# Building a gate table from one-hot pairs: one float32 VectorE operation per eight tokens, a stepped PSUM tile, and 62 parked chunks in place of 48

## The chip, the cores and the metric

The kernel runs on one core of a Trainium2 chip. The engines are TensorE (PE for its matmuls, PEld for its weight loads), VectorE (DVE), ScalarE (ACT), GpSimd (POOL) and SyncE (SP, which here issues the plain DMAs). The metric is the device time of one execution in microseconds, lower is better.

## The reference, cut to what matters

One encoder block over 512 tokens of width 1024. What this text is about is its last big part, a product-key retrieval over 128 x 128 = 16384 single-neuron experts, 8 heads with 16 experts each, so that every token has 128 experts and 128 gates:

```python
top_s, pos = lax.top_k(cand, K)
idx = jnp.take_along_axis(cand_idx, pos, axis=-1)      # i1 * 128 + i2
g = jax.nn.softmax(top_s, axis=-1)
...
ue = jnp.take(u, ib, axis=0)
a = jnp.einsum('thkd,td->thk', ue, xb)
w = jax.nn.gelu(a) * gb
ve = jnp.take(v, ib, axis=0)
return jnp.einsum('thk,thkd->td', w, ve)
```

## The kernel before, in words

The first third of the program (input projections, attention, the recurrent branch, the merge) is not touched. Then the 512 tokens of the retrieval are split: the first 128 are done as the reference does it, with gathered rows of u and v (an indirect DMA on the POOL queue, then a DVE product: `gu`, `gv`, lines 885, 891, 900). The other 384 tokens are done densely: for all 16384 experts, in 128 chunks of 128 experts, the kernel computes gelu(u x), multiplies it with a gate table that is zero where an expert was not chosen, and multiplies the result with v.

A **chunk** on the first side is `dense_a` (line 776 on): one load of 512 KB (`u_raw`), its split into two parts (`u_h` on ACT, line 139; `u_l` on DVE, line 140), 24 matmuls of 128 x 384 into the PSUM tile `pa` (lines 134 to 136), and a Gelu on ACT to `ge` (line 784). On the second side (`w_prep` and `w_mm`) a chunk takes the split of `v_raw`, a product with the gate table (line 1003), a split into `w_h` and `w_l`, and 18 matmuls of 128 x 512 into `po`.

**The gate table** has for each of the 384 tokens a 128 x 128 matrix: entry (i, j) is the gate of expert 128 i + j. `build` makes it as a product of two one-hot matrices. For a block of 128 tokens the chosen i, j and gates are transposed (`tij`, `gr`: token along the free axis, choice along the partitions). Then, for 8 tokens at a time (`TQ`):

- DVE compares: `gL` (line 865), 8 x 128 float32, from a constant `iob` that holds 0..127 in bfloat16 with every value 8 times in a row, read with a step; and `gO` (line 867), 128 x 8 bfloat16, with the 8 tokens innermost;
- ACT scales one token's slice of `gO` by the gates into `gR` (line 869), one instruction for each token, which reads with a step of 8 elements;
- PE multiplies `gR` and `gL` of one token into `pg` (line 874), four tokens in a PSUM tile, each with its 128 columns side by side. A float32 matmul of the program is two matmul instructions in the profile, so there are 768 of them for 384 tokens;
- ACT copies `pg` to `gs` (line 876) and turns it there, so that the token is innermost.

After 32 tokens (`GB`), `gs` (one buffer) goes to memory in one DMA of 2 MB (line 878): 12 such blocks in all, four for each of the three blocks of 128 tokens.

While the table is not finished, no `po` matmul can run. So the table's work is interleaved with `dense_a` of the first `SP` chunks, whose results are **parked** in memory (`adram<-ge`, line 958) and read back in the last stage (`ges<-adram`). The other 128 - `SP` chunks are **fresh**: their `dense_a` is done among the `po` matmuls of the last stage. Generators set the program order: `units()` zips the selection of the experts (`sel`, `topk`: many small DVE operations) of one block with the `build` of another, each step with a cost; whenever the cost passes another multiple of `APACE`, one more `dense_a` is issued (`next_a`), and the gathers come in at a pace of their own (`GPACE`). A scheduler then places the instructions of each engine; each engine and each DMA queue runs its own in that order.

Of the kernel before, what the change touches and what calls it, by code (L numbers as in the profile page):

```python
# [8 lines left out]
F32 = mybir.dt.float32  # L9
F32R = mybir.dt.float32r  # L10
BF16 = mybir.dt.bfloat16
I32 = mybir.dt.int32
U32 = mybir.dt.uint32
AF = mybir.ActivationFunctionType
OP = mybir.AluOpType
# [31 lines left out]
TD = T - NG  # L47
NTB = TD // GB
PRE = 8
SP = 48  # L50
TQ = 8
APACE = 3.3
GPACE = 0.4
GSTART = 30
GS2 = 135
# [22 lines left out]
def chunk_order():  # L78
    spilled, fresh = [], []
    for c in range(128):  # L80
        ns, nf = SP - len(spilled), 128 - SP - len(fresh)
        (spilled if ns and (c < S0 or not nf or ns * (128 - SP) >= nf * SP) else fresh).append(c)
    return {c: i for i, c in enumerate(spilled)}, spilled + fresh
# [29 lines left out]
def zipped(*gens):  # L113
    gens = [[0.0, i, g] for i, g in enumerate(gens)]
    while gens:
        e = min(gens)
        try:
            c = next(e[2])
        except StopIteration:
            gens.remove(e)  # L120
            continue
        e[0] += c
        yield c
# [633 lines left out]
def peer(nc, tc, I, out, xd, cst, gains, norm_T1, rstd_of, split, mm3, tap, stop, pp, ha, la, h2n, v8s, i8s, st, top,  # L757
         idxg, gg, acc, aa, ul_st, up, u_split, u_pre):
    import contextlib
    V, S, PE, G, DM = nc.vector, nc.scalar, nc.tensor, nc.gpsimd, nc.sync  # L760
    ident = cst[:, C_ID:C_ID + 128]
    iota = cst[:, C_IOTA:C_IOTA + 128]
# [3 lines left out]
    if True:  # L766
        dp = st.enter_context(tc.tile_pool(name="gdram", bufs=1, space=bass.MemoryType.DRAM))
        gd = dp.tile([NTB, 128, 128 * GB], F32, name="gdram")
        ad = dp.tile([SP, 128, TD], F32, name="adram")
        ys = contextlib.ExitStack()  # L770
# [76 lines left out]
            V.tensor_tensor(g3, g3, sm[:, :, None].to_broadcast([128, 8, 16]), op=OP.mult)  # L847
            yield 0.6

        def build(kp, bp, ps, tb, i_f, g_o, iob):  # L850
            pt = ps.tile([128, 3, 128], F32, name="pt3", tag="pt3", bufs=1)
            for i, s in enumerate((i_f[:, 0, :], i_f[:, 1, :], g_o)):
                PE.transpose(pt[:, i, :], s, ident)
            tij = kp.tile([128, 2, 128], BF16, name="tij", tag="tij")
            S.activation(tij, pt[:, 0:2, :], AF.Copy)
            gr = kp.tile([128, 128], F32, name="gr", tag="gr")
            S.activation(gr, pt[:, 2, :], AF.Copy)
            for b in range(128 // GB):
                gs = bp.tile([128, 128, GB], F32, name="gs", tag="gs", bufs=1)
                for q8 in range(GB // TQ):  # L860
                    t0 = b * GB + q8 * TQ
                    LL = bp.tile([128, TQ, 128], F32, name="gL", tag="gL")
                    OO = bp.tile([128, 128, TQ], BF16, name="gO", tag="gO")
                    RR = bp.tile([128, TQ, 128], F32, name="gR", tag="gR")
                    V.tensor_tensor(LL, iob[:, :, 0][:, None, :].to_broadcast([128, TQ, 128]),
                                    tij[:, 0, t0:t0 + TQ, None].to_broadcast([128, TQ, 128]), op=OP.is_equal)
                    V.tensor_tensor(OO, iob, tij[:, 1, None, t0:t0 + TQ].to_broadcast([128, 128, TQ]), op=OP.is_equal)  # L867
                    for t in range(TQ):
                        S.activation(RR[:, t, :], OO[:, :, t], AF.Copy, scale=gr[:, t0 + t:t0 + t + 1])  # L869
                    for q4 in range(TQ // 4):  # L870
                        pg = ps.tile([128, 4, 128], F32, name="pg", tag="pg")
                        for w in range(4):
                            t = q4 * 4 + w
                            PE.matmul(pg[:, w, :], RR[:, t, :], LL[:, t, :], start=True, stop=True)  # L874
                        o = q8 * TQ + 4 * q4
                        S.activation(gs[:, :, o:o + 4].rearrange("p i t -> p t i"), pg, AF.Copy)  # L876
                    yield TQ * 0.21 + 0.1
                DM.dma_start(gd[(tb - TB0) * (128 // GB) + b], gs.rearrange("p i t -> p (i t)"))

# [40 lines left out]
        with s7:  # L920
            kp = s7.enter_context(tc.tile_pool(name="topk", side="right", **LR))
            bp = s7.enter_context(tc.tile_pool(name="gbld", side="right", bufs=2, reuse_waits="tile"))
            ps = s7.enter_context(tc.psum_pool(name="psg", side="right", bufs=2, reuse_waits="tile"))
            iob = kp.tile([128, 128, TQ], BF16, name="iob")
            V.tensor_copy(iob, iota[:, :, None].to_broadcast([128, 128, TQ]))
            i16 = kp.tile([128, 16, NK], BF16, name="i16")
            V.tensor_copy(i16, iota[:, 0:16, None].to_broadcast([128, 16, NK]))

            def sel(tb):
                i_f = kp.tile([128, 2, NK], F32, name="i_f", tag="i_f", bufs=2)  # L930
                g_o = kp.tile([128, NK], F32, name="g_o", tag="g_o", bufs=2) if tb >= TB0 else gg
                sels[tb] = i_f, g_o
                yield from topk(kp, tb, i_f, g_o, i16)
                if tb < TB0:
                    idx_f = kp.tile([128, NK], F32, name="idx_f", tag="idx_f")
                    V.scalar_tensor_tensor(idx_f, i_f[:, 0, :], 128.0, i_f[:, 1, :], op0=OP.mult, op1=OP.add)
                    V.tensor_copy(idxg, idx_f)
                    tap("idx", idx_f)
                    tap("g", gg)

            sels = {}

            def units():
                yield from sel(0)
                yield from sel(1)
                for tb in (1, 2, 3):
                    gens = [build(kp, bp, ps, tb, *sels[tb], iob)]
                    if tb < 3:
                        gens.append(sel(tb + 1))
                    yield from zipped(*gens)  # L950

            na, cost = 0, 0.0
            pend = []

            def next_a(c):
                ge = dense_a(c)
                if c < SP:
                    DM.dma_start(ad[c], ge)
                else:
                    pend.append(ge)  # L960

            for _ in range(A0):
                next_a(na)
                na += 1
            for u in units():
                cost += u
                while cost > (na + 1 - A0) * APACE and na < SP + NPE:
                    next_a(na)
                    na += 1
                if cost > GSTART:  # L970
                    gathers((cost - GSTART) * GPACE + max(0.0, cost - GS2) * GP2, None)
            GW = cnt["u"]
            print("COST", cost, na, GW) if DBG else None
            while na < SP + NPE:
                next_a(na)
                na += 1
# [123 lines left out]
        with contextlib.ExitStack() as e2:  # L1100
            pe2.append(e2.enter_context(tc.tile_pool(name="ple3", side="right", **LR)))
            ps = e2.enter_context(tc.psum_pool(name="psp", side="right", bufs=4, reuse_waits="tile"))
            for n in range(4):
                w = wg0 if n == 0 else load_wg(n)
# [60 lines left out]
```

## Time and profile before

| what | value |
|---|---|
| median of 3 runs | 1922.45 us (1918.22 to 1923.83) |
| the profiled execution's own time | 1921.56 us |
| its span | 1919.8 us |
| mean granted TensorE clock | 0.994 |
| PE, DVE, ACT, POOL busy | 1841.0, 1416.3, 982.5, 374.3 us |
| first and last `pg` matmul | 687.8 and 1001.6 us |
| first `po` matmul of the last stage | 1026.8 us |

The profile gives, for a stretch of the span, each engine's busy time, the granted clock, the mean share of the DMA engines and their GB/s. Its groups of instructions have the busy time, the mean duration of one, and what ended the idle time before them. Matmuls overlap in their pipeline: one is shown with 0.28 to 0.39 us where the next starts 0.12 to 0.23 us after it. So a PE that is shown as busy can still do more, and its cost is read from start to start.

### The profile page before, as it was taken

How to read it: one execution, taken by the hardware profiler on the slowest of the kernel's cores; microseconds unless marked ns; L12 is line 12 of the kernel's file. 1: busy time of each engine (PE TensorE's matmuls, PEld its weight loads, DVE VectorE, ACT ScalarE, POOL GpSimd, SP SyncE). 2: the span in 40 equal slices, each digit the busy share in tenths (PEclk: the TensorE clock that was granted, in tenths of full speed). 3: DMA queues.
4: the chain of work that ended last, by engine and by line, in shares of the span. 5: the costliest groups of instructions: out<-in, count | busy, mean ns of one | idle time of the engine just before them, and what ended most of it. 6: DMA issues, size and time to landing. Idle time of an engine off the chain costs nothing.

```text
span 1919.8 us, 27163 instructions
## 1 busy us (share of the span) xinstructions
PE 1841.0 (96%) x9989; PEld 1619.2 (84%) x9989; DVE 1416.3 (74%) x2893; ACT 982.5 (51%) x1561; POOL 374.3 (19%) x260
## 2 busy tenths in 40 slices
PE   6999999999999999888889999999999999999998
PEld 5997888888887988787778888888888888888888
DVE  3689787444898999988746778887777777656464
ACT  5755656432433589999994334333333333333443
POOL 0000000000000322214301334443354443201000
PEclk9999999999999999999999999999999999999999
DMA  4212100433321776777748998988999988765512
GB/s 161 78 55 78 45 12 23 132 108 129 119 84 60 268 252 239 270 262 266 260 168 307 335 338 318 326 327 319 327 332 341 319 306 324 265 220 177 191 58 86
DMA packets 133941, 397.44 MB, mean 207 GB/s; under 512 B 12848, under 2 KB 52016, under 8 KB 132144
## 3 DMA queue, kind: packets, MB, share of 16 engines
q1 hardware_dynamic: 96944, 261.48, 38.7%
q0 software_dynamic: 36864, 134.23, 19.6%
q8 instruction: 78, 1.28, 0.3%
q14 instruction: 55, 0.45, 0.1%
HBM read 356.86 MB, written 38.80 MB: 206 GB/s over the span
## 4 chain that ended last, share of the span: by engine, by line
PE 45%; ACT 9%; DMA 2%; DVE 1%; issue 0%; ACTq 0%; SPq 0%
PE po L136 9%; PE po L135 9%; PE po L134 9%; PE pa L136 5%; PE pa L135 5%; PE pa L134 5%; ACT gR L869 4%; ACT gs L876 3%; DMA gdram<-gs 1%; ACT u_h L139 1%; PE pg L134 1%; PE pg L136 1%; PE pg L135 1%; DMA gchg<-gdram 1%; ACT ge L784 0%
## 5 line engine op out<-in xcount | busy, mean ns | idle before, releaser
L885 POOL DMA_INDIRECT gu<-in_peer_u_dram,idxg x128 | 191.7, 1498 | 1131.8 <-DVE cd L808 659.5
L136 PE MATMUL pa<-ha,u_l 128*128 128x384 f32 x1024 | 349.4, 341 | 5.5 <-DVE u_l L140 5.5
L134 PE MATMUL pa<-ha,u_h 128*128 128x384 f32 x1024 | 349.3, 341 | 2.2 <-ACT u_h L139 1.8
L135 PE MATMUL pa<-la,u_h 128*128 128x384 f32 x1024 | 348.7, 341 | 0.0
L134 PE MATMUL po<-v_h,w_h 128*128 128x512 f32 x768 | 299.5, 390 | 1.9 <-ACT w_h L139 1.9
L135 PE MATMUL po<-v_l,w_h 128*128 128x512 f32 x768 | 300.8, 392 | 0.0
L136 PE MATMUL po<-v_h,w_l 128*128 128x512 f32 x768 | 300.7, 392 | 0.0
L139 ACT ACTIVATE u_h<-u_raw 128x1024 fp32r<-128x1024 f32 x128 | 136.4, 1066 | 205.8 <-PE pa L135 198.2
L885 POOL DMA_INDIRECT gv<-in_peer_v_dram,idxg x128 | 182.4, 1425 | 239.9 <-DVE acc L900 208.2
L140 DVE TENSOR_TENSOR u_l<-u_raw,u_h 128x1024 fp32r<-128x1024 f32 x128 | 156.2, 1221 | 90.7 <-ACT u_h L139 90.6
L136 PEld LDWEIGHTS pa<-ha,u_l 128*128 128x128 f32 x1024 | 193.3, 189 | 7.6 <-DVE u_l L140 7.4
L134 PEld LDWEIGHTS pa<-ha,u_h 128*128 128x128 f32 x1024 | 193.5, 189 | 6.0 <-ACT u_h L139 2.5
L135 PEld LDWEIGHTS pa<-la,u_h 128*128 128x128 f32 x1024 | 193.3, 189 | 2.8
L874 PE MATMUL pg<-gL,gR 128*128 128x128 f32 x768 | 145.7, 305 | 34.8 <-ACT gs L876 18.3
L140 DVE TENSOR_TENSOR v_l<-v_raw,v_h 128x1024 fp32r<-128x1024 f32 x128 | 155.9, 1219 | 25.5 <-ACT v_h L139 25.5
L869 ACT ACTIVATE gR<-gO,gr 128x128 f32<-128x128 bf16 x384 | 170.0, 547 | 4.1 <-DVE gO L867 4.0
L134 PEld LDWEIGHTS po<-v_h,w_h 128*128 128x128 f32 x768 | 144.5, 188 | 30.8 <-ACT w_h L139 2.2
L136 PEld LDWEIGHTS po<-v_h,w_l 128*128 128x128 f32 x768 | 144.6, 188 | 30.3
L874 PEld LDWEIGHTS pg<-gL,gR 128*128 128x128 f32 x768 | 108.4, 191 | 71.9 <-ACT gR L869 33.5
L135 PEld LDWEIGHTS po<-v_l,w_h 128*128 128x128 f32 x768 | 144.5, 188 | 28.7
L900 DVE SCALAR_TENSOR_TENSOR acc<-gv,aa,acc 128x1024 f32<-128x1024 f32 x128 | 163.7, 1279 | 5.3 <-DMA gv<-in_peer_v_dram,idxg 4.9
L891 DVE SCALAR_TENSOR_TENSOR gu<-gu,h2n 128x1024 f32<-128x1024 f32 x128 | 155.5, 1217 | 6.5 <-DMA gu<-in_peer_u_dram,idxg 6.5
(323 smaller groups left out, 3448.7 us busy)
## 6 DMA issues: line engine op xcount, KB each, us to landing
u_raw<-in_u_t_dram SPq DMA_DIRECT2D x128, 512.0 KB, 5.4
v_raw<-in_peer_v_dram SPq DMA_DIRECT2D x128, 512.0 KB, 6.7
gdram<-gs SPq DMA_DIRECT2D x12, 2048.0 KB, 7.8
gchg<-gdram SPq DMA_DIRECT2D x16, 1536.0 KB, 12.6
w_raw<-in_w_in_dram SPq DMA_DIRECT2D x42, 512.0 KB, 3.6
adram<-ge SPq DMA_DIRECT2D x48, 192.0 KB, 3.3
ges<-adram SPq DMA_DIRECT2D x48, 192.0 KB, 6.5
wq_raw<-in_peer_wq_dram SPq DMA_DIRECT2D x16, 512.0 KB, 3.5
```

What stands on the lines that cost most here:

```text
L134: PE.matmul(ps, lh, rh, start=first, stop=False)
L135: PE.matmul(ps, lh, rl, start=False, stop=False)
L136: PE.matmul(ps, ll, rh, start=False, stop=last)
L139: ins = S.activation(hi, raw, AF.Copy)
L140: V.tensor_tensor(lo, raw, hi.bitcast(F32), op=OP.subtract)
L869: S.activation(RR[:, t, :], OO[:, :, t], AF.Copy, scale=gr[:, t0 + t:t0 + t + 1])
L874: PE.matmul(pg[:, w, :], RR[:, t, :], LL[:, t, :], start=True, stop=True)
L876: S.activation(gs[:, :, o:o + 4].rearrange("p i t -> p t i"), pg, AF.Copy)
L885: G.indirect_dma_start(out=t, out_offset=None, in_=src, in_offset=bass.IndirectOffsetOnAxis(ap=idxg[:, k:k + 1], axis=0))
L891: V.scalar_tensor_tensor(t, t, 1.0, h2n, op0=OP.mult, op1=OP.mult, accum_out=aa[:, k:k + 1])
L900: V.scalar_tensor_tensor(acc, t, aa[:, k:k + 1], acc, op0=OP.mult, op1=OP.add)
```

## The change

The constant `iob` goes. The indices `tij` are kept in float32. One DVE operation writes both one-hots of 8 tokens as `gE`, 2 x 8 x 128 float32, each token's 128 values side by side, in place of `gL` and `gO`. ACT reads a contiguous slice of `gE` for `gR`. The PSUM tile `pg` becomes 128 x 4: the matmul of one token writes its 128 columns with a step of 4, so that four tokens lie innermost, and the ACT copy to `gs` reads `pg` in order and writes runs of four. The number of parked chunks goes from 48 to 62, and `APACE` from 3.3 to 2.6.

```diff
-SP = 48
+SP = 62
 TQ = 8
-APACE = 3.3
+APACE = 2.6
...
-            tij = kp.tile([128, 2, 128], BF16, name="tij", tag="tij")
+            tij = kp.tile([128, 2, 128], F32, name="tij", tag="tij")
...
                 for q8 in range(GB // TQ):
                     t0 = b * GB + q8 * TQ
-                    LL = bp.tile([128, TQ, 128], F32, name="gL", tag="gL")
-                    OO = bp.tile([128, 128, TQ], BF16, name="gO", tag="gO")
+                    EE = bp.tile([128, 2, TQ, 128], F32, name="gE", tag="gE")
                     RR = bp.tile([128, TQ, 128], F32, name="gR", tag="gR")
-                    V.tensor_tensor(LL, iob[:, :, 0][:, None, :].to_broadcast([128, TQ, 128]),
-                                    tij[:, 0, t0:t0 + TQ, None].to_broadcast([128, TQ, 128]), op=OP.is_equal)
-                    V.tensor_tensor(OO, iob, tij[:, 1, None, t0:t0 + TQ].to_broadcast([128, 128, TQ]), op=OP.is_equal)
+                    V.tensor_tensor(EE, iota[:, None, None, :].to_broadcast([128, 2, TQ, 128]),
+                                    tij[:, :, t0:t0 + TQ, None].to_broadcast([128, 2, TQ, 128]), op=OP.is_equal)
                     for t in range(TQ):
-                        S.activation(RR[:, t, :], OO[:, :, t], AF.Copy, scale=gr[:, t0 + t:t0 + t + 1])
-                    for q4 in range(TQ // 4):
-                        pg = ps.tile([128, 4, 128], F32, name="pg", tag="pg")
+                        S.activation(RR[:, t, :], EE[:, 1, t, :], AF.Copy, scale=gr[:, t0 + t:t0 + t + 1])
+                    for q in range(TQ // 4):
+                        pg = ps.tile([128, 128, 4], F32, name="pg", tag="pg")
                         for w in range(4):
-                            t = q4 * 4 + w
-                            PE.matmul(pg[:, w, :], RR[:, t, :], LL[:, t, :], start=True, stop=True)
-                        o = q8 * TQ + 4 * q4
-                        S.activation(gs[:, :, o:o + 4].rearrange("p i t -> p t i"), pg, AF.Copy)
+                            t = 4 * q + w
+                            PE.matmul(pg[:, :, w], RR[:, t, :], EE[:, 0, t, :], start=True, stop=True)
+                        o = q8 * TQ + 4 * q
+                        S.activation(gs[:, :, o:o + 4], pg, AF.Copy)
...
-            iob = kp.tile([128, 128, TQ], BF16, name="iob")
-            V.tensor_copy(iob, iota[:, :, None].to_broadcast([128, 128, TQ]))
```

The instructions move on the engines. On PE, in the third group of eight tokens of the first block, the rows before are these (`pg` is the table, `pa` a chunk's matmuls):

```order
L136 MATMUL pa<-ha,u_l 128x384
L874 MATMUL pg<-gL,gR 128x128
L134 MATMUL pa<-ha,u_h 128x384
L874 MATMUL pg<-gL,gR 128x128 x3
L135 MATMUL pa<-la,u_h 128x384
L874 MATMUL pg<-gL,gR 128x128 x2
L136 MATMUL pa<-ha,u_l 128x384
L874 MATMUL pg<-gL,gR 128x128
L134 MATMUL pa<-ha,u_h 128x384
```

and now, for the same group of tokens:

```order
L134 MATMUL pa<-ha,u_h 128x384
L135 MATMUL pa<-la,u_h 128x384
L136 MATMUL pa<-ha,u_l 128x384
L872 MATMUL pg<-gE,gR 128x128 x8
L134 MATMUL pa<-ha,u_h 128x384
L135 MATMUL pa<-la,u_h 128x384
L136 MATMUL pa<-ha,u_l 128x384
```

The eight tokens of a group now stand together more often. Over the whole table PE goes 156 times from `pa` to `pg` and back before, and 96 times now. Between the first and the last `pg` stand 35.3 chunks of `pa` before and 46.5 now; ahead of the first `pg` 16.4 and 17.4; between the last `pg` and the first `po` 5.4 and 5.3; after the first `po` 70.9 and 58.8.

On ACT, at the start of the first block, the rows before are these (`gR` is the scaled one-hot, `gs` the copy out of PSUM, `ge` and `u_h` belong to chunks):

```order
L869 ACTIVATE gR<-gO,gr 128x128
L876 ACTIVATE gs<-pg 128x4x128
L869 ACTIVATE gR<-gO,gr 128x128 x7
L876 ACTIVATE gs<-pg 128x4x128
L869 ACTIVATE gR<-gO,gr 128x128
L139 ACTIVATE u_h<-u_raw 128x1024
L784 ACTIVATE ge<-pa 128x384
```

and now:

```order
L867 ACTIVATE gR<-gE,gr 128x128
L874 ACTIVATE gs<-pg 128x128x4
L867 ACTIVATE gR<-gE,gr 128x128 x4
L139 ACTIVATE u_h<-u_raw 128x1024
L784 ACTIVATE ge<-pa 128x384
L867 ACTIVATE gR<-gE,gr 128x128 x3
L874 ACTIVATE gs<-pg 128x128x4
```

The `u_h` and `ge` of a chunk stand after fewer `gR` than before: between the first `gR` and the last `gs` there are 35 pairs of them before and 46 now. The counts of `gR` (384) and `gs` (96) do not change. On DVE, 43 of the 128 gathered products `gu` stand in the first eight blocks of the table before, and 51 now.

More of the change, by code (lines that the diff above doesn't have):

```diff
@@ L848, in topk, with build @@
             yield 0.6
-        def build(kp, bp, ps, tb, i_f, g_o, iob):
+        def build(kp, bp, ps, tb, i_f, g_o):
             pt = ps.tile([128, 3, 128], F32, name="pt3", tag="pt3", bufs=1)
@@ L946, in units @@
                 for tb in (1, 2, 3):
-                    gens = [build(kp, bp, ps, tb, *sels[tb], iob)]
+                    gens = [build(kp, bp, ps, tb, *sels[tb])]
                     if tb < 3:
```

## The prediction

> **What bounds the kernel now.** I read the page first. PE is busy for 96% of the span, so time can only come from where PE idles or runs below its pace. The stretches of the retrieval show where (columns: length, then busy time and instructions of PE, PEld, DVE, ACT, POOL, the clock, the DMA share, GB/s):
>
> ```profile
> PE 1841.0 (96%) x9989; PEld 1619.2 (84%) x9989; DVE 1416.3 (74%) x2893; ACT 982.5 (51%) x1561; POOL 374.3 (19%) x260
> ...
> 640.00:688.00 48.00, 45.35 (x252) 42.89 (x251) 46.88 (x157) 26.77 (x33) 17.21 (x14) 1.00 0.85 310
> 688.00:906.00 218.00, 196.57 (x1136) 171.68 (x1136) 197.57 (x392) 207.59 (x381) 65.00 (x43) 0.99 0.72 252
> 906.00:1002.00 96.00, 82.67 (x489) 70.75 (x488) 64.03 (x60) 92.38 (x181) 15.69 (x10) 1.00 0.60 221
> 1002.00:1030.00 28.00, 25.73 (x138) 24.44 (x137) 13.39 (x17) 12.99 (x18) 0.00 (x0) 0.95 0.81 283
> 1030.00:1826.00 796.00, 796.00 (x3891) 707.62 (x3890) 580.74 (x721) 289.17 (x411) 276.19 (x190) 1.00 0.83 298
> ```
>
> From 688 to 1002 the gate table is built, its first eight blocks up to 906, the last four after. ACT is busy for 300 of these 314 us, PE for 279. From 1030 to 1826 PE is never idle. So ACT bounds the table and PE the last stage. The waits of the table say the same: PE waits for ACT.
>
> ```profile
> PEld pg L874 <- ACT gR L869: 33.1, 60, 1.5
> PEld pg L874 <- ACT gs L876: 24.9, 23, 2.3
> PE pg L874 <- ACT gs L876: 18.3, 19, 2.0
> PE pg L874 <- ACT gR L869: 15.1, 45, 1.2
> DVE gL L865 <- PE pg L874: 14.9, 18, 2.7
> ```
>
> The true pace is in the timelines of PE and ACT (start, length, instruction):
>
> ```profile
> 965.70 0.33 PE L134 MATMUL pa<-ha,u_h 128*128 128x384 f32 x1
> ...
> 968.47 0.34 PE L135 MATMUL pa<-la,u_h 128*128 128x384 f32 x1
> 970.69 2.05 PE L874 MATMUL pg<-gL,gR 128*128 128x128 f32 x16 [1.88 <-ACT gs L876]
> ...
> 977.32 0.42 PE L135 MATMUL pa<-la,u_h 128*128 128x384 f32 x1
> 977.58 0.81 PE L874 MATMUL pg<-gL,gR 128*128 128x128 f32 x4
> 978.14 0.42 PE L136 MATMUL pa<-ha,u_l 128*128 128x384 f32 x1
> ...
> 885.73 6.41 ACT L869 ACTIVATE gR<-gO,gr 128x128 f32<-128x128 bf16 x15
> 892.04 0.47 ACT L784 ACTIVATE ge<-pa 128x384 f32<-128x384 f32 x1
> 892.41 1.05 ACT L139 ACTIVATE u_h<-u_raw 128x1024 fp32r<-128x1024 f32 x1
> 893.36 1.96 ACT L876 ACTIVATE gs<-pg 128x512 f32<-128x512 f32 x2
> 895.11 1.34 ACT L869 ACTIVATE gR<-gO,gr 128x128 f32<-128x128 bf16 x3
> ```
>
> From 965.70 to 968.47 lie 16 steps of `pa`: 0.173 us each, 4.16 us for a chunk of 24. The 16 `pg` in 2.05 us, less some 0.28 for the last one's length, give 0.118 each. One `pa` and four `pg` take 0.82 (977.32 to 978.14) where 0.173 + 4 x 0.118 = 0.645, so each turn from `pa` to `pg` and back costs 0.175. On ACT a `gR` takes 6.31 / 15 = 0.42, a `gs` 1.75 / 2 = 0.88 here, some 0.92 over several pairs, a `ge` with its `u_h` 0.37 + 0.95 = 1.32.
>
> ACT's need for the table: 384 x 0.42 + 96 x 0.92 + 35 x 1.32 + 11 of small ones = 307 of 314. PE's: 35.3 x 4.16 + 768 x 0.118 + 1.4 (transposes) = 239, and 156 turns x 0.175 = 27, so 266. PE loses 314 - 266 = 48 us to waits.
>
> **The change on ACT.** The nearest rows:
>
> ```profile
> L869 ACT ACTIVATE gR<-gO,gr 128x128 f32<-128x128 bf16 x384 | 170.0, 547 | 4.1 <-DVE gO L867 4.0
> L189 ACT ACTIVATE ha<-pt_n,gains 128x128 fp32r<-128x128 f32 x64 | 21.4, 364 | 19.1 <-PE pt_n L184 11.5 <-DVE la L190 6.7
> L876 ACT ACTIVATE gs<-pg 128x512 f32<-128x512 f32 x96 | 103.7, 1126 | 3.3 <-DMA gdram<-gs 2.2 <-PE pg L874 1.0
> L741 ACT ACTIVATE sc<-psc 128x512 f32<-128x512 f32 x16 | 9.6, 599 | 20.6 <-issue 15.6 <-PE psc L739 5.1
> ```
>
> A scaled copy of the same size without a step takes 364 ns, from PSUM, with the scale per partition as here. Instructions overlap by some 0.1, so `gR` goes from 0.42 to between 0.26 and 0.42; I take 0.28, near the row of the same form. `gs` now writes runs of four where it wrote single elements 128 bytes apart; a plain copy takes 599 ns, so between 0.5 and 0.92; I take 0.5. ACT then needs 384 x 0.28 + 96 x 0.5 + 46 x 1.32 + 11 = 227 (all at the upper ends: 321). It stops being the bound, unless both stay as they are, and then the table takes 321 + 7 = 328 us.
>
> **On DVE.**
>
> ```profile
> L865 DVE TENSOR_TENSOR gL<-iob,tij 128x1024 f32<-128x1024 bf16 x48 | 96.4, 2007 | 16.1 <-PE pg L874 14.9 <-ACT tij L855 1.1
> L867 DVE TENSOR_TENSOR gO<-iob,tij 128x1024 bf16<-128x1024 bf16 x48 | 32.8, 683 | 13.0 <-ACT gR L869 12.9
> L140 DVE TENSOR_TENSOR u_l<-u_raw,u_h 128x1024 fp32r<-128x1024 f32 x128 | 156.2, 1221 | 90.7 <-ACT u_h L139 90.6
> L830 DVE TENSOR_TENSOR ri<-ri,hit 128x128 f32<-128x128 f32 x32 | 9.1, 284 | 0.0
> L891 DVE SCALAR_TENSOR_TENSOR gu<-gu,h2n 128x1024 f32<-128x1024 f32 x128 | 155.5, 1217 | 6.5 <-DMA gu<-in_peer_u_dram,idxg 6.5
> ```
>
> `gL` and `gO` cost 2.69 us together. `gE` has 2048 float32 elements; from 284 ns (128) and 1221 ns (1024) an element costs 1.05 ns, so `gE` costs 1221 + 1024 x 1.046 = 2.29 (lower end), or 2 x 2.007 = 4.01 if `gL`'s price comes from the repeated operand and not from the step of `iob`. I take 2.29: `gL` is the only float32 product that reads with such a step. In the first eight blocks DVE then has 197.6 - 32 x 0.40 + 10.1 more `u_l` x 1.22 + 8 more `gu` x 1.3 = 207. Behind a `gE` that waits stand these `u_l`, `gu` and the selection of the next block; PE waits for `u_l`.
>
> **On PE, in the table.** 46.5 chunks x 4.16 + 90.6 + 1.4 = 285, and 96 turns x 0.175 = 17: 302. Of this the first eight blocks have 36.7 x 4.16 + 512 x 0.118 + 64 x 0.175 = 224, so PE is ahead of DVE (207) there, by little. Of the 48 us of waits I keep 12, a quarter (bounds 0 and 48): a `gR` still has to come before its `pg`, and `gs` has one buffer, whose DMA takes 7.8 us to land, 12 times. The table takes 314 us again: **0** (-12 to +36), with 11.1 more chunks in it.
>
> The `pg` matmuls now write with a step of four. No row has a stepped PSUM output, so the price is open, from 0 up to the rival below. I take 0, for this row:
>
> ```profile
> L566 PE MATMUL poa<-akv,PTt 128*128 128x64 f32 x256 | 32.3, 277 | 0.0
> ```
>
> With 64 columns a matmul still takes 32.3 / 256 = 0.126: at 128 columns the pace of 0.118 is not set by the columns that it writes, so part of a slower write is covered.
>
> **Ahead of the table** stands one chunk more: 4.2 us of PE in a stretch (640 to 688) where PE has 2.7 free and DVE 1.1, and the constant `iob` (0.7 on DVE) is gone: **+3** (0 to +4).
>
> **The last stage** has 70.9 - 58.8 = 12.1 chunks less. PE is the bound without a gap, so 12.1 x 4.16 = **-50**. Its DVE and ACT lose 12 splits too. The parked results take 14 more writes of 192 KB on the SP queue, and 14 more reads, in front of `v_raw` loads; 12 loads of 512 KB go. The DMA engines have less time for nearly the same bytes:
>
> ```profile
> 1050.00:1075.00 25.00, 25.00 (x112) 20.71 (x111) 22.82 (x34) 9.97 (x20) 13.00 (x9) 1.00 1.00 378
> 1130.00:1330.00 200.00, 200.00 (x992) 179.32 (x991) 155.42 (x195) 71.15 (x101) 86.00 (x61) 1.00 0.90 321
> 1330.00:1530.00 200.00, 200.00 (x991) 179.29 (x990) 157.77 (x198) 71.61 (x101) 92.50 (x61) 1.00 0.91 331
> ```
>
> At a share of 1.00 they move 378 GB/s. The stage gets shorter by 50 / 796, and 331 becomes some 331 x 1.067 x 0.985 = 348, which is 92% of that. It fits, but loads that come in bursts will be late at times: **+3** (0 to +15). Between the last `pg` and the first `po` the same 5.3 chunks cover the table's way through memory: 0.
>
> **The sum**, against the profiled execution (1921.56, of it 1919.8 the span): 1921.6 + 3 + 0 - 50 + 3 = 1877.4. That execution lies 0.9 under the median, well inside the spread of the runs, so I take **1877 us**, with a range of its own of 1862 to 1902.
>
> **The rivals.** *The stepped PSUM write.* If each of the 768 matmuls takes twice its step, 0.236, the table's PE need is 302 + 90.6 = 393, ACT and DVE wait for it, and the table takes 79 us more: 1921.6 + 3 + 79 - 50 = **1953**, slower. It decides from (44 + 12) / 768 = 0.073 us for each matmul on. For it: nothing in the trace writes so. Against: the row of `poa`. The Trainium skill (PSUM — Partial Sum Buffer, Specifications) speaks for this rival: it gives PSUM cachelines of 8 bytes and says that any non-contiguous access pattern slows matmuls significantly. The step here is 16 bytes; no run so far shows what that costs.
>
> *The waits stay.* PE's order still ties each `pg` to a `gR`, and all 48 us remain, now for DVE or for the single `gs`: 1877 + 36 = **1913**. For it: DVE at 207 of some 230 us in the first blocks. Against: most of the waits shown name ACT, which becomes 80 us shorter. If ACT keeps both its prices, 328 instead of 314 gives 1891; this lies between.
>
> *DVE becomes the bound.* With `gE` at 4.01 DVE has 207 + 32 x 1.72 = 262 us in the first eight blocks, 38 over PE's 224, and part of its old idle time of 20 on top: 1877 + 45 = **1922**, no change. Against: `gE` reads no step.
>
> *The DMA engines become the bound* of the last stage: 1877 + 12 = 1889, inside the range.
>
> **How the numbers follow.** 0.60 for 1877 with its own range, 0.16 for waits or ACT in between (1891 to 1913), 0.05 for DVE and no change, 0.17 for the stepped write, 0.02 for the rest. A measurement of this kernel tells about 0.3% (6 us) from no change. Faster: 0.60 + 0.16 + 0.02 = 0.78; same 0.05; slower 0.17. The range has to leave out no more than 0.2: from 1859 (no waits, no DMA loss) to 1925, which takes in all but the stepped write at its full price.
>
> **What would show it.** Right: `gR` near 0.36 us, `gs` near 0.6, `gE` near 2.3; a row of 16 `pg` in about 2.05 us; ACT well under PE between the first and the last `pg`, that stretch still some 314 us long; PE at 100% in the last stage, which ends some 50 us earlier. Wrong: a `pg` step above 0.15 (the rival), a longer table in which PE waits for DVE or for the DMA of `gs`, or PE idle after 1030 behind `v_raw` or `ges`.

## The result and the profile after

| | before | after |
|---|---|---|
| median | 1922.51 us (1918.22 to 1923.83) | 1892.66 us (1890.1 to 1895.21) |
| the profiled execution's span | 1919.8 us | 1890.9 us |
| mean granted clock | 0.994 | 0.991 |
| first to last `pg` of the table | 687.8 to 1001.6: 313.8 us | 690.2 to 992.8: 302.6 us |
| last stage, first `po` to first `pg<-wg_h` | 1026.8 to 1837.4: 810.6 us | 1015.4 to 1808.8: 793.4 us |

The ratio is 0.9849, with a 95% interval of 0.9828 to 0.9869: about 30 us faster. The forecast was 1877, with 1862 to 1902 as its own range, so the sign and the range held, but some 15 of the 45 us forecast did not come.

The span is 28.9 us shorter, and the marks of the table above split that: +2.4 ahead of the table, -11.2 in the table, -2.6 between its end and the first `po`, -17.2 in the last stage, -0.3 behind it. The forecast had +3, 0, 0 and -47. So the table gave 11 us that were not expected, and the last stage kept back some 30.

The marks come from the rows of the tiles (duration min/median/max in ns, then first and last start) of the kernel after:

```profile
L872 PE MATMUL pg<-gE,gR x768: 270/275/422, 690.2 to 992.8; 128*128 128x128 f32 x192
...
L134 PE MATMUL pg<-wg_h,ha x128: 277/283/388, 1808.8 to 1886.2; 128*128 128x256 f32 x128
```

The stretches of the kernel after have the columns of the prediction's first fence:

```profile
690.00:900.00 210.00, 197.91 (x1275) 194.16 (x1273) 197.96 (x365) 155.41 (x373) 79.29 (x49) 0.99 0.84 300
900.00:993.00 93.00, 92.07 (x617) 89.71 (x618) 56.55 (x34) 81.44 (x211) 3.18 (x3) 0.98 0.62 229
1018.00:1118.00 100.00, 100.00 (x469) 86.10 (x468) 84.92 (x116) 39.92 (x61) 40.32 (x30) 1.00 0.96 353
1118.00:1218.00 100.00, 100.00 (x491) 88.97 (x490) 78.10 (x99) 35.24 (x51) 51.76 (x31) 1.00 0.93 340
...
1418.00:1518.00 100.00, 91.00 (x423) 80.52 (x422) 68.00 (x87) 31.08 (x43) 42.16 (x27) 0.95 0.80 283
1518.00:1618.00 100.00, 88.29 (x398) 77.72 (x397) 66.21 (x84) 28.46 (x40) 33.96 (x24) 0.93 0.78 276
1618.00:1718.00 100.00, 97.60 (x477) 86.35 (x476) 62.57 (x78) 34.87 (x49) 19.29 (x14) 1.00 0.73 256
```

In the table (the first two rows) PE is now busy for 290 of 303 us and ACT for only 237: ACT is no longer the bound. PE now comes nearest to being it; up to 900 DVE is as busy as PE, and these rows alone do not tell the two apart there. In the last stage PE is full until some 1418. From there on it idles for 23 us in 300, and the granted clock falls to 0.95 and 0.93. Before, PE was at 100% through the whole stage.

The waits of the last stage (total, times, longest) tell who was late:

```profile
ACT v_h L139 <- DMA v_raw<-in_peer_v_dram: 122.3, 37, 12.9
...
DVE ges L999 <- DMA ges<-adram: 91.4, 23, 9.2
...
PE pa L136 <- DVE u_l L140: 23.1, 8, 5.0
```

In the kernel before the first two were

```profile
ACT v_h L139 <- DMA v_raw<-in_peer_v_dram: 20.6, 11, 4.4
...
DVE ges L1003 <- DMA ges<-adram: 17.0, 7, 6.4
```

and PE never waited for `u_l` there. Now PE waits for `u_l`, which is a fresh chunk's split on DVE, and DVE waits for `ges`, a parked chunk that is read back. One such place in the timeline, first of the SP queue, then DVE, then PE:

```profile
1444.41 0.33 SPq L996 DMA_DIRECT2D ges<-adram  x1
```

```profile
1443.83 0.55 DVE L140 TENSOR_TENSOR w_l<-ges,w_h 128x384 fp32r<-128x384 f32 x1
1444.30 1.21 DVE L140 TENSOR_TENSOR v_l<-v_raw,v_h 128x1024 fp32r<-128x1024 f32 x1
1450.88 0.56 DVE L999 TENSOR_TENSOR ges<-ges,gchg 128x384 f32<-128x384 f32 x1 [5.37 <-DMA ges<-adram]
1451.36 1.22 DVE L889 SCALAR_TENSOR_TENSOR gu<-gu,h2n 128x1024 f32<-128x1024 f32 x1
...
1452.50 1.22 DVE L140 TENSOR_TENSOR u_l<-u_raw,u_h 128x1024 fp32r<-128x1024 f32 x1
```

```profile
1453.78 0.62 PE L136 MATMUL pa<-ha,u_l 128*128 128x384 f32 x1 [4.97 <-DVE u_l L140]
1454.20 0.52 PE L134 MATMUL pa<-ha,u_h 128*128 128x384 f32 x1
1454.52 0.52 PE L135 MATMUL pa<-la,u_h 128*128 128x384 f32 x1
```

`w_l` is the last reader of a `ges` buffer. The next read-back is issued when it ends (1444.41), lands 6.5 us later, and DVE stands on it for 5.37 us with `u_l` behind it. Then PE has idled for 4.97 us, and its next `pa` start 0.32 us apart, up to 1457.08, where they were 0.173 apart before.

### The profile page after: what moved, and what is told of

It reads as the page before. It is cut to its first block, busy times and chain, and to the rows that moved or that the text cites. A ratio compares the mean times of both kernels' runs of the same rounds, so it can differ in the third digit from the quotient of the medians.

```text
span 1890.9 us, 27215 instructions
## 1 busy us (share of the span) xinstructions
PE 1811.2 (96%) x9989; PEld 1618.7 (86%) x9989; DVE 1394.3 (74%) x2844; ACT 901.9 (48%) x1561; POOL 385.4 (20%) x260
## 4 chain that ended last, share of the span: by engine, by line
PE 74%; DVE 13%; DMA 7%; ACT 2%; issue 2%; POOL 0%; SPq 0%; DVEq 0%; ACTq 0%; POOLq 0%
PE po L135 8%; PE po L136 8%; PE po L134 8%; PE pa L136 6%; PE pa L135 6%; PE pa L134 6%; PE pg L872 4%; PE pT L134 3%; PE pT L135 3%; PE pT L136 3%; DMA ges<-adram 3%; DVE u_l L140 2%; PE poa L566 2%; PE pq L134 2%; PE pq L135 2%
## 5 line engine op out<-in xcount | busy, mean ns | idle before, releaser
L134 PE MATMUL pa<-ha,u_h 128*128 128x384 f32 x1024 | 353.4, 345 | 1.8 <-ACT u_h L139 1.8
L883 POOL DMA_INDIRECT gv<-in_peer_v_dram,idxg x128 | 192.6, 1505 | 224.1 <-DVE acc L898 194.8
L139 ACT ACTIVATE v_h<-v_raw 128x1024 fp32r<-128x1024 f32 x128 | 134.3, 1052 | 144.2 <-DMA v_raw<-in_peer_v_dram 123.0
L867 ACT ACTIVATE gR<-gE,gr 128x128 f32<-128x128 f32 x384 | 122.1, 393 | 32.8 <-DVE gE L864 32.6
L999 DVE TENSOR_TENSOR ges<-ges,gchg 128x384 f32<-128x384 f32 x62 | 34.0, 554 | 137.3 <-DMA ges<-adram 91.4
```

Source lines behind the costliest of these rows:

```text
L134: PE.matmul(ps, lh, rh, start=first, stop=False)
L139: ins = S.activation(hi, raw, AF.Copy)
L867: S.activation(RR[:, t, :], EE[:, 1, t, :], AF.Copy, scale=gr[:, t0 + t:t0 + t + 1])
L883: G.indirect_dma_start(out=t, out_offset=None, in_=src, in_offset=bass.IndirectOffsetOnAxis(ap=idxg[:, k:k + 1], axis=0))
L999: mi = V.tensor_tensor(ge.rearrange("p (b t) -> p b t", t=GB), ge.rearrange("p (b t) -> p b t", t=GB), gch[key][:, :, c % GC, :], op=OP.mult)
```

## The experiments

Theory A: the table gained, and the last stage lost because 62 parked chunks are more than it can read back in time. Theory B: the new table's order spoils the last stage. Within A there were three: A1, the four `ges` buffers (`B_GE`) make the read-backs late; A2, the DMA engines are full; A3, DVE's queue is full.

All runs in one place. "Table" goes from the first to the last `pg`, "stage" from the first `po` to the first `pg<-wg_h`, both from the profiled execution. The ratio is to the kernel before on the same chip; that kernel took between 1918.8 and 1922.5 us on the chips used, so times of different rows compare only to some 4 us, and ratios better.

| run | us | ratio (95%) | table | stage |
|---|---|---|---|---|
| before | 1922.5 | 1 | 313.8 | 810.6 |
| after | 1892.7 | 0.9849 (0.9828 to 0.9869) | 302.6 | 793.4 |
| new table, 48 parked | 1863.5 | 0.9713 (0.9695 to 0.9730) | 263.9 | 808.1 |
| old table, 62 parked | 1946.5 | 1.0150 (1.0133 to 1.0166) | 352.9 | 795.2 |
| after, plain PSUM tile | 1908.4 | 0.9939 (0.9919 to 0.9959) | 315.8 | 793.3 |
| after, 5 `ges` buffers | 1877.0 | 0.9782 (0.9765 to 0.9798) | 303.3 | 783.8 |
| after, half the `gv` gathers | 1872.6 | 0.9749 (0.9732 to 0.9767) | 302.5 | 776.8 |
| after, half the `acc` sums | 1887.4 | 0.9833 (0.9814 to 0.9852) | 304.0 | 785.9 |
| after, 55 parked | 1857.4 | 0.9678 (0.9659 to 0.9697) | 280.5 | 783.4 |
| after, 8 `ges`, 5 gel buffers | 1860.1 | 0.9679 (0.9658 to 0.9701) | 305.4 | 759.5 |
| after, 5 gel buffers | 1891.4 | 0.9846 (0.9827 to 0.9866) | 305.4 | 790.8 |
| before, stepped PSUM tile | 1888.5 | 0.9834 (0.9819 to 0.9849) | 286.0 | 808.9 |
| new one-hots, plain PSUM, 48 | 1886.0 | 0.9815 (0.9800 to 0.9830) | 289.3 | 807.3 |
| 55 parked, 8 `ges`, 5 gel | 1864.9 | 0.9700 (0.9682 to 0.9718) | 282.0 | 791.2 |

### The new table alone

```diff
-SP = 62
-APACE = 2.6
+SP = 48
+APACE = 3.3
```

> The new table with the old 48 parked chunks and their old pace (APACE 3.3). Nothing of the computation is left out. Theory A (the last stage lost its gain because 62 parked chunks read back are more than its buffers and DMA engines carry; the table itself gained): the last stage is that of the kernel before, PE 100% in its windows, about 799 us; the table has 14 parked products less in PE, 302.6 - 14 x 4.16 = 244 us where PE alone counts, and at least DVE's and ACT's own work, which puts it at 255 to 280 us. Whole kernel 1922 - (34 to 59) = 1865 to 1888, not slower than the changed kernel's 1893. Theory B (the table's new order delays something that the last stage needs, whatever the parking): the last stage shows PE idle there here too, and the kernel is above 1890.

1863.5 us, ratio 0.9713: below the lower end of A's 1865 by 1.5 us, and 29 us faster than the whole change (26 by the ratios). Its last stage, in the windows of this run:

```profile
1450.00:1550.00 100.00, 100.00 (x498) 89.76 (x497) 76.93 (x95) 35.16 (x49) 49.49 (x30) 1.00 0.89 320
1550.00:1650.00 100.00, 100.00 (x492) 89.14 (x491) 72.47 (x88) 35.17 (x49) 27.06 (x19) 1.00 0.80 280
```

PE idles nowhere and the clock is 1.00, with the new table in place. Theory B falls. The table takes 263.9 us, 49.9 less than before, with as many parked chunks. It even holds a little more: 906 `pa` matmuls start between the first and the last `pg`, which is 37.8 chunks of 24, where the kernel before has 35.3.

### The parking alone

```diff
-SP = 48
-APACE = 3.3
+SP = 62
+APACE = 2.6
```

made in the kernel before.

> The old table (two one-hots apart, bfloat16 indices) with 62 parked chunks at the pace of 2.6. Nothing of the computation is left out. Theory A (62 parked chunks cost the last stage some 33 us of PE idle and low clock whatever the table does): the table grows from 313.8 us, by 14 products of 4.16 us less what PE had idle there, so by 15 to 35 us; the last stage is again about 782 us rather than the 749 that 12 products less would leave; in all 1922 + (15 to 35) - 17 = 1920 to 1940. Theory B (the loss comes with the new table): the last stage falls by 50 us and the kernel comes to 1887 to 1907.

1946.5 us, ratio 1.015: slower than before, and above A's range by 6 us, since the table grew by 39.1 us where 15 to 35 were expected. Its last stage is 795.2 us, and its windows show the same picture as the change's:

```profile
1450.00:1550.00 100.00, 91.73 (x431) 81.65 (x431) 69.85 (x89) 32.05 (x44) 43.87 (x28) 0.95 0.85 301
1550.00:1650.00 100.00, 90.53 (x421) 79.95 (x420) 64.70 (x80) 28.68 (x40) 37.68 (x27) 0.95 0.81 286
```

So the loss in the last stage belongs to the 62 parked chunks. The two halves nearly add: -2.87% and +1.50%, together -1.37%, where the whole change has -1.51%. The parking costs the table as much in the old one (39.1 us) as in the new (302.6 - 263.9 = 38.7). Not all 14 chunks go there: between the first and the last `pg` the new table has 37.8 chunks with 48 parked and 46.5 with 62, the old one 35.3 and 45.7 (1097 matmuls). So a further chunk costs 4.4 us in the new table and 3.8 in the old, which is about PE's own 4.16: the waits took in next to nothing of it.

### The stepped PSUM write undone

```diff
-                        pg = ps.tile([128, 128, 4], F32, name="pg", tag="pg")
+                        pg = ps.tile([128, 4, 128], F32, name="pg", tag="pg")
...
-                            PE.matmul(pg[:, :, w], RR[:, t, :], EE[:, 0, t, :], start=True, stop=True)
+                            PE.matmul(pg[:, w, :], RR[:, t, :], EE[:, 0, t, :], start=True, stop=True)
...
-                        S.activation(gs[:, :, o:o + 4], pg, AF.Copy)
+                        S.activation(gs[:, :, o:o + 4].rearrange("p i t -> p t i"), pg, AF.Copy)
```

> The changed kernel with one part undone: the four pg matmuls of a group write each its own contiguous 128 columns of PSUM again, and ScalarE's copy turns them (a read stepped by 512 bytes). Nothing of the computation is left out. If the stepped PSUM write cost TensorE nothing: pg's step stays at 0.12 us, gs goes from 0.59 back to about 1.1 us, ScalarE has 96 x 0.5 = 48 us more in a table in which it was below VectorE and PE, and the kernel stays within 1893 to 1910. If the stepped write cost TensorE something: pg's 384 matmuls get shorter and the table with them, by up to 384 x 0.118 = 45 us, and the kernel is below 1890.

1908.4 us (1899.5 to 1913.4), inside the range for a write that costs nothing, and the table is 13.2 us longer. (The copy that turns reads `pg` in order and writes single elements 128 bytes apart; it does not read by steps, as the expectation has it.) Whether the write by steps costs PE anything is told by rows of 16 `pg` without a gap, in the timeline of the kernel after:

```profile
706.60 1.95 PE L872 MATMUL pg<-gE,gR 128*128 128x128 f32 x16
```

and of this run with the plain tile:

```profile
704.43 1.95 PE L872 MATMUL pg<-gE,gR 128*128 128x128 f32 x16
```

Both take 1.95 us, some 0.11 for each. The groups of the table, first after, then with the plain tile, show the other side (busy us, mean ns of one, then idle time before it):

```profile
L867 ACT ACTIVATE gR<-gE,gr 128x128 f32<-128x128 f32 x384 | 122.1, 393 | 32.8 <-DVE gE L864 32.6 <-ACT gs L874 0.2
L864 DVE TENSOR_TENSOR gE<-cst,tij 128x2048 f32<-128x2048 f32 x48 | 109.2, 2284 | 16.0 <-PE pg L872 16.0
L872 PE MATMUL pg<-gE,gR 128*128 128x128 f32 x768 | 106.1, 282 | 6.5 <-ACT gs L874 3.3 <-issue 2.5 <-ACT gR L867 0.5
...
L874 ACT ACTIVATE gs<-pg 128x512 f32<-128x512 f32 x96 | 55.5, 590 | 14.1 <-DMA gdram<-gs 8.1 <-PE pg L872 4.8 <-issue 0.8
```

```profile
L872 PE MATMUL pg<-gE,gR 128*128 128x128 f32 x768 | 110.5, 287 | 17.9 <-ACT gs L874 14.5 <-ACT gR L867 2.6
...
L874 ACT ACTIVATE gs<-pg 128x512 f32<-128x512 f32 x96 | 101.8, 1108 | 13.2 <-DMA gdram<-gs 11.3 <-PE pg L872 1.8
```

The copy goes from 590 back to 1108 ns, 50 us in 96 copies, and PE's wait for it from 3.3 to 14.5. The 11 us more of that wait are most of the table's 13.

### A fifth read-back buffer

```diff
-B_GE = 4
+B_GE = 5
```

> The changed kernel with a fifth buffer for the parked chunks that are read back in the last stage (B_GE 5 instead of 4), nothing else. Nothing of the computation is left out. Theory A1 (read-backs are issued too late, each only once the fourth chunk before is split, and VectorE's queue stands on their landing for 5 us): VectorE's wait for them (91 us) falls by a third or more, PE's wait for u_l with it, and the kernel comes to 1870 to 1885. Theory A2 (the DMA engines are full in the first 400 us of the stage and what they are behind comes due later): the wait moves to v_raw or gchg, and the kernel stays within 1888 to 1896.

1877.0 us, 15.7 less (13 by the ratios), inside A1's range. The waits for read-backs in the last stage, total, times, longest:

```profile
DVE ges L999 <- DMA ges<-adram: 49.6, 15, 10.0
...
PE pa L136 <- DVE u_l L140: 17.1, 6, 6.7
```

DVE's wait is nearly halved, PE's is a quarter less. What this leaves open is whether the rest is the same cause or the engines.

### Fewer transfers, and less work for DVE

Half the gathers (the odd slots take the rows of the one before):

```diff
-            t = gather(vn, k, "gv")
+            if k % 2 == 0:
+                half[0] = gather(vn, k, "gv")
+            t = half[0]
```

> The changed kernel, but only every second gv gather is made; the other half of the sums takes the rows of the gather before once more. Left out are 64 transfers of 0.52 MB, 33 MB of the last stage's some 250; VectorE does all its operations, so the sums for half the slots are of other rows. Theory A2 (the last stage loses time because the DMA engines are at 0.92 to 0.97 in its first 400 us and the loads come later and later): PE's idle time and the low clock after 1400 us go, and the kernel comes to 1855 to 1868. Theory A3 (VectorE's queue is what is full, and a load's landing only shows it): no transfer is waited for that VectorE would not have made wait, and the kernel stays within 1882 to 1893.

Half the sums:

```diff
-            V.scalar_tensor_tensor(acc, t, aa[:, k:k + 1], acc, op0=OP.mult, op1=OP.add)
+            n = D if k % 2 == 0 else 64
+            V.scalar_tensor_tensor(acc[:, 0:n], t[:, 0:n], aa[:, k:k + 1], acc[:, 0:n], op0=OP.mult, op1=OP.add)
```

> The changed kernel, but every second addition of a gathered gv row to acc takes 64 of its 1024 columns only, so that half the slots are missing in most columns. All transfers are made. VectorE has 64 x (1.28 - some 0.1) = 75 us less in the last stage. Theory A3 (VectorE's queue is what is full): PE's wait for u_l goes and the kernel comes to 1855 to 1870. Theory A2 (the DMA engines): the loads land as late as before, PE waits as before, and the kernel stays within 1885 to 1896.

1872.6 us with half the gathers: 20 less than the change, between the ranges of A2 and A3. Its windows show that the idle time is not the DMA engines' being full at that point:

```profile
1450.00:1550.00 100.00, 90.79 (x424) 79.37 (x422) 65.42 (x82) 30.96 (x45) 29.23 (x18) 0.97 0.73 252
1550.00:1650.00 100.00, 96.22 (x464) 85.45 (x464) 76.21 (x96) 34.00 (x47) 21.11 (x14) 0.98 0.72 245
```

PE still idles for 13 us while the engines are busy for 0.73 of the time. Fewer transfers bring each load in earlier (a read-back lands after a median of 5.5 us here, 6.6 with five buffers). DVE's wait for read-backs falls from 91.4 us to 68.5 and does not go, and the stage gets 16.6 us shorter (793.4 to 776.8), about half of what the change lost in it. With half the sums it is 1887.4 us, inside A2's range, and that interval overlaps the change's own: 61 us of DVE's busy time gone (1394 to 1334 us) bring some 3 to 5 us, if anything. The wait stays, in that run's last stage:

```profile
DVE ges L1000 <- DMA ges<-adram: 101.5, 23, 11.5
```

A3 falls. Fuller DMA engines make the loss larger (A2), but by these two runs they are not shown to be all of it.

### Eight read-back buffers, and the control

`PRE` is the number of `ge` buffers (the gel pool), into which every chunk's first side is written; the room for four more `ges` was taken from it.

```diff
-PRE = 8
+PRE = 5
...
-B_GE = 4
+B_GE = 8
```

> The changed kernel with eight buffers for read-back chunks instead of four, and the products' own buffers (gel) cut from 8 to 5 to make room. Nothing of the computation is left out. Theory A1 (four buffers make the read-backs late; a fifth brought 16 us): VectorE's wait for read-backs goes below 25 us and the kernel comes to 1858 to 1870. Theory A2 or A3 (engines that are full): the waits stand elsewhere, at v_raw and gchg, and the kernel stays within 1872 to 1885.

> The changed kernel with its products' own buffers (gel) cut from 8 to 5 and the read-backs left at four: the other half of the edit that took the kernel to 1860. Nothing of the computation is left out. Theory A1 (the read-back buffers alone made that gain): 1888 to 1897, as the changed kernel, with PE idle after 1440. If the shorter gel pool made it, by holding fresh products back: 1858 to 1870.

The buffers bring the kernel to 1860.1 us; the shorter gel pool by itself leaves it at 1891.4, where the change is. So the buffers did it. The last stage takes 759.5 us, 51.1 less than before. In its windows PE is full to the end:

```profile
1018.00:1118.00 100.00, 100.00 (x469) 86.20 (x468) 84.34 (x115) 40.65 (x62) 39.25 (x29) 1.00 0.97 361
1418.00:1518.00 100.00, 100.00 (x490) 88.90 (x489) 76.19 (x97) 32.57 (x45) 46.99 (x31) 1.00 0.93 337
1518.00:1618.00 100.00, 99.54 (x486) 88.05 (x486) 83.31 (x107) 38.57 (x55) 42.17 (x27) 1.00 0.90 316
```

The row of DVE's wait for `ges<-adram` is gone from its waits altogether. DVE still waits for the gate table's slices (`gchg`: 69.4 us in this row, 45.8 in the same row of the change) and ACT for `v_raw`, but PE hardly waits for `u_l` any more:

```profile
DVE ges L999 <- DMA gchg<-gdram: 69.4, 11, 9.3
...
ACT v_h L139 <- DMA v_raw<-in_peer_v_dram: 52.3, 23, 8.5
...
PE pa L136 <- DVE u_l L140: 0.3, 1, 0.3
```

The DMA engines move more here (361 and 337 GB/s in the first two rows, where the change has 353 and 283), and what still waits for them does not hold PE up. Theory A1 stands: with four buffers a read-back was issued too late, and everything behind it on DVE came late too, `v_l` and the next `v_raw` load among them.

### 55 parked chunks

```diff
-SP = 62
-APACE = 2.6
+SP = 55
+APACE = 2.93
```

> The changed kernel with 55 parked chunks at a pace of 2.93, halfway between the 48 and 62 tried so far. Nothing of the computation is left out. If the last stage's loss starts at a threshold (its buffers and engines still carry 55): the table is halfway, 264 + 19 = 283 us, the last stage 25 us shorter than with 48, at PE 100%, so 1863 + 19 - 29 + some 2 = 1853 to 1860. If the loss grows with every parked chunk: 1872 to 1885, between the two.

1857.4 us, inside the range for a threshold: PE is at 100% in every window of the last stage up to 1750, with four buffers; one of them is

```profile
1550.00:1650.00 100.00, 100.00 (x495) 89.55 (x494) 70.13 (x87) 35.90 (x50) 26.69 (x19) 1.00 0.80 276
```

DVE still waits 35.9 us for read-backs there, in 13 waits, and that does not reach PE. The table takes 280.5 us (283 expected). This run is the fastest of all runs together with the eight buffers (the two intervals overlap), and 1.7% faster than the change (0.9678 / 0.9849 = 0.983). What sets the threshold between 55 and 62 was not tried.

```diff
-PRE = 8
-SP = 62
+PRE = 5
+SP = 55
...
-APACE = 2.6
+APACE = 2.93
...
-B_GE = 4
+B_GE = 8
```

> 55 parked chunks and eight read-back buffers together (gel 5). Nothing of the computation is left out. Theory A1: with 55 chunks PE was already at 100% through the last stage, so there is nothing left for the buffers to give, and the kernel stays at 1853 to 1860, with no more than 4 us to the run with 55 and four buffers. If read-back waits still cost something with 55: below 1850.

1864.9 us, above the range: 7.6 more than with 55 alone, but 0.2% (4 us) by the ratios, whose intervals overlap. The traces show more than the medians do, since the profiled execution is the slowest of its five here and was the fastest of its four there. The first `po` comes 5.3 us later (993.0 against 987.7), and 3.6 of that stand ahead of the table already (first `pg` at 688.5 against 684.9). Ahead of the first `po` is a wait that the other run lacks, and behind it more `pa`:

```profile
L134 PE MATMUL po<-v_h,w_h 128*128 128x512 f32 x731 | 285.7, 391 | 5.1 <-ACT w_h L139 5.1
L136 PE MATMUL pa<-ha,u_l 128*128 128x384 f32 x528 | 177.2, 336 | 0.0
```

and with 55 parked and eight gel buffers it is

```profile
L136 PE MATMUL pa<-ha,u_l 128*128 128x384 f32 x521 | 174.9, 336 | 0.0
```

So about one chunk less stands ahead of the first `po` and one more in the last stage (7 or 8 matmuls of each kind, 7 x 3 x 0.173 = 3.6 us). The shorter gel pool, which holds chunks back, may be the reason; with 55 parked chunks it was not tried alone, so this is not shown. What the run does show is that with 55 the eight buffers bring nothing.

### The two halves of the table

The stepped PSUM tile alone, in the kernel before:

```diff
-                        pg = ps.tile([128, 4, 128], F32, name="pg", tag="pg")
+                        pg = ps.tile([128, 128, 4], F32, name="pg", tag="pg")
...
-                            PE.matmul(pg[:, w, :], RR[:, t, :], LL[:, t, :], start=True, stop=True)
+                            PE.matmul(pg[:, :, w], RR[:, t, :], LL[:, t, :], start=True, stop=True)
...
-                        S.activation(gs[:, :, o:o + 4].rearrange("p i t -> p t i"), pg, AF.Copy)
+                        S.activation(gs[:, :, o:o + 4], pg, AF.Copy)
```

> The kernel before with one part of the change alone: four tokens innermost in PSUM, so that gs is copied without a turn. 48 parked chunks, the two old one-hots. Nothing of the computation is left out. ScalarE has 96 x (1.13 - 0.59) = 52 us less in a table that it sets; VectorE keeps 2.69 us for each eight tokens, against 2.28 in the new table that lasts 264 us. Theory C (ScalarE set the old table, and behind it VectorE is next): the table comes to 264 + 48 x 0.41 = 284 us and the kernel to 1922 - 30 = 1885 to 1898. Theory D (PE's write to PSUM by steps costs what ScalarE saves): pg's matmuls get longer and the table stays within 305 to 320 us, the kernel within 1912 to 1928.

The new one-hots alone (the run with the plain tile, and besides):

```diff
-SP = 62
-APACE = 2.6
+SP = 48
+APACE = 3.3
```

> The new one-hots alone: gE by one VectorE operation in float32 and the contiguous gR, with the plain PSUM tile and its turning copy, and 48 parked chunks. Nothing of the computation is left out. ScalarE has 384 x 0.154 = 59 us less, VectorE 48 x 0.41 = 20 us. Theory C: ScalarE is no longer alone the bound; the table comes to 264 us plus the 13 us that the turning copy cost with 62 chunks, 270 to 285 us, and the kernel to 1868 to 1892. If the float32 one-hots gave nothing and the PSUM order all of the table's gain: 1912 to 1925.

1888.5 and 1886.0 us, both inside Theory C's ranges for the kernel; the tables are 286.0 (284 expected) and 289.3 (270 to 285 expected, so 4 too long). They save 27.8 and 24.5 us, together 52.3, and both at once saved 49.9. In the first the table holds as many `pa` as before, and the work taken off ACT (some 52 us) was about twice the gain: a saved microsecond on ACT gave half a microsecond, so ACT's busy time was never the whole of the old table's pace. In the second 59 us went from ACT and 20 from DVE, but 2.4 chunks (10 us of PE) more stand in the table, so its 24.5 us is no clean price. Theory D falls with the first of the two. Its timeline has

```profile
899.67 0.82 PE L874 MATMUL pg<-gL,gR 128*128 128x128 f32 x4
```

and the run with the new one-hots and the plain tile

```profile
934.38 0.61 PE L872 MATMUL pg<-gE,gR 128*128 128x128 f32 x4
```

Four `pg` among single `pa` take 0.82 with the old one-hots and 0.61 with the new, whichever way PSUM is written.

## Why the prediction was right, and where its sum was off

**The number** fell into the range in part by luck. The forecast had 0 for the table and -47 for the last stage; measured are -11 and -17. Without the 11 us of the table the kernel would have taken 1904 us, outside the range of 1862 to 1902: two errors of opposite sign met. The source of the gain is another than forecast, too. It was to come from the chunks moved out of the last stage, for which the faster table only made room; but the new table alone, with 48 parked, saves 2.9%, and moving 14 more gives 1.4 of these points back.

**ACT's prices** held. `gR` was put near 0.36 us and shows 0.393; fifteen in a row take 4.50 us in the table after, from 938.32 on, so (4.50 - 0.39) / 14 = 0.29 from start to start, where 0.28 was taken:

```profile
938.32 4.50 ACT L867 ACTIVATE gR<-gE,gr 128x128 f32<-128x128 f32 x15
```

`gs` was put near 0.6 and shows 0.590. ACT is busy for 237 us of the table (227 forecast), and no longer its bound.

**DVE's price** held: 2.284 us for `gE` (2.29 forecast, bound 4.01). That rival falls: `gL`'s 2.007 us for half the elements came from its operands in the old form, not from the repeat that `gE` has too. Whether their step or their type did it was not tried.

**The stepped PSUM write** was priced at 0, and that is what it costs: 1.95 us for 16 with it and without. The rival of 1953 falls. The Trainium skill (PSUM — Partial Sum Buffer, Specifications) says that any non-contiguous access pattern slows matmuls significantly; for this write, 128 float32 columns 16 bytes apart, the measurement does not bear it out.

**The table's 0** was -11.2. The forecast had 302 us for PE, of which 285 were matmuls and 17 were 96 turns from `pa` to `pg` at 0.175 us, and 12 us of waits on top. By the same prices 302.6 - 285 = 17 us are left for turns and waits together, where 17 + 12 = 29 were put. The term that failed is the turn. It was worked out from 0.82 us for one `pa` and four `pg` (977.32 to 978.14). Four `pg` are two tokens, and each token needs a `gR`. ACT's row at that moment, in the kernel before, is

```profile
976.54 2.13 ACT L869 ACTIVATE gR<-gO,gr 128x128 f32<-128x128 bf16 x5
```

With 0.49 us for a single one, these five start (2.13 - 0.49) / 4 = 0.41 us apart, so two take 0.82: PE kept ACT's pace there. The same piece takes 0.63 in the kernel after (940.15 to 940.78):

```profile
940.15 0.61 PE L872 MATMUL pg<-gE,gR 128*128 128x128 f32 x4
940.51 0.42 PE L136 MATMUL pa<-ha,u_l 128*128 128x384 f32 x1
940.78 0.60 PE L872 MATMUL pg<-gE,gR 128*128 128x128 f32 x4
```

It lies within the fifteen `gR` shown above, 0.29 apart, of which two take 0.59, so PE may keep ACT's pace here as well. A turn then costs at most 0.63 - (0.173 + 4 x 0.11) = 0.02 us, and 96 of them 2 us instead of 17. The two runs with half a table each show that the 0.82 goes with the old one-hots. So the prediction booked a wait for ACT as a price of PE, and kept it for a kernel in which ACT is faster. This is read from the traces; no run changed `gR`'s time and nothing else. It also made the old waits too small: without turns they are 314 - 239 = 75 us, not 48. A quarter of 75 is 19, close to the 17 that are left now.

**The parked chunks in the table** were to cost nothing, since PE's waits would take them in. They cost 38.7 us with the new table and 39.1 with the old, about what PE needs for them. In the forecast this stands hidden: 0 for the table was a gain of 50 and a loss of 39 together, and neither was priced by itself.

**The last stage's -50** is what PE has less to do there: 51.1 us came off with eight `ges` buffers. In the change as it stands 17.2 came off. The term that was mis-sized is the +3 (0 to +15) for transfers, which measured about +33: 23 us of PE's idle time, and some 11 us more of its busy time at the lower clock around these waits. It was sized by bandwidth (348 of 378 GB/s, and the change did reach 353 in its first 100 us), and bandwidth alone was not what failed: the run with eight buffers moves more and loses nothing. What was missing is the number of buffers. The prediction counted 14 more read-backs, but not that each waits for one of four `ges` buffers, that DVE takes its work in order, and that `u_l` and `v_l` stand behind the wait. "PE idle after 1030 behind `v_raw` or `ges`" was named as what would show it wrong, and that is what the trace has.

**The rivals.** "The waits stay" (1913) did not come: at most 17 us of waits are left in the table. The DMA engines as the bound of the last stage gave 1889, near the measured 1893, but by another way: leaving out half of the `gv` gathers took away half of the stage's loss, and eight buffers, with every transfer made, took away all of it.

## What to carry to other kernels

When a change moves work from one stage to another, price both ends by themselves. Here a moved chunk cost the new table 4.4 us, and the last stage could win no more than PE's 4.16 for it. With four buffers 48 or 55 parked chunks were better than 62, and even with eight buffers, where the last stage won all that it could, 62 came out within some 5 us of 48 (1860.1 and 1863.5). So nearly all of the gain was the faster table. When a change adds loads, count the buffers that they go through and find what stands behind the waiting instruction on its engine, before the bandwidth. And a pace read from a timeline of an engine that waits for another is that other engine's pace: it must not be kept as a price once the other is sped up.

## What was not expected of the hardware

- A matmul of 128 x 128 in float32 that writes its 128 columns 16 bytes apart in PSUM takes the same time as one that writes them side by side (1.95 us for 16 in both).
- After a wait of 4.97 us PE's `pa` started 0.32 us apart instead of 0.173, and the mean granted clock was 0.95 and 0.93 over the two stretches of 100 us in which PE idled for 9 and 12 us, and 1.00 in the other stretches shown of the last stage. The idle time cost about half as much again: 23 us idle, and 11 us more of busy time (770.1 us of PE in the last stage, 758.8 in the run with eight buffers, for the same matmuls).
- ACT's copy out of PSUM took 590 ns when it wrote runs of 16 bytes and read in order, and 1108 to 1126 ns when it read in order and wrote single elements 128 bytes apart; scaling 128 elements took 393 ns from contiguous float32 and 547 from bfloat16 with a step of 16 bytes.
